# The second-layer coefficients of token blocks 1, 6 and 7 move to a pool of their own, opened after the constants of the attention are closed

## Chip, cores and metric

The kernel runs on one core of one Trainium2 chip. The metric is device microseconds of one execution; the spans and rows below come from one profiled execution. The engines are TensorE (PE: matmuls; PEld: its weight loads), VectorE (DVE), ScalarE (ACT), GpSimd (POOL, which here only issues gathers) and SyncE (SP, which issues the other transfers).

## What is computed

One encoder layer on 1024 tokens of width 1024: two attentions, a gated merge, and a retrieval of single-neuron experts (PEER). The change touches the last part:

```python
def peer(xn, wq, keys, u, v):          # per token: 8 heads x 16 experts = 128 of 16384
    ...                                # top 16 of two key halves, top 16 of their sums -> e, g
    ue = u[e]                          # first layer: 128 rows of 1024 floats per token
    ve = v[e]                          # second layer: 128 rows of 1024 floats per token
    hid = einsum('thkd,td->thk', ue, xb)
    a = gelu(hid) * g
    return einsum('thk,thkd->td', a, ve)
```

## The kernel before

The tokens are eight blocks of 128. For blocks 2 to 5 (`DBLK`) the experts are computed densely: `gates` turns the chosen experts into a matrix of gate values (DVE lines L653 and L663, ACT lines L660, L661 and L671, PE line L669), and `dense_experts` then multiplies by all of `u` and `v` on PE. For blocks 0, 1, 6 and 7 (`SBLK`) `experts(b)` gathers. POOL issues 256 gathers of 128 rows (512 KB each, L803) for a block, in order: 128 from `u`, 128 from `v`. Each `u` gather is reduced on DVE by one instruction (`junk`, L809) to one column of `hid`. When all 128 columns are there, ACT makes `a` = gelu(`hid`) (L811), DVE multiplies it by `g` (L812), and each `v` gather is added by one DVE instruction into `acc` (L815, `acc += a[:,k] * ge`). The gathered tiles `ge` have 5 buffers; a buffer is free again when its DVE instruction is done.

Before the dense stage stand, in this order: the projections with the attention of blocks 0 to 3; the attention of blocks 4 to 7 (`att_rest`: scores L347 on PE, masks and minima L353 on DVE, exponentials L360 on ACT, products L372 on PE); then the merge of blocks 4 and 5 with the gates of blocks 2 and 3 (`mop(2)`); then the choice of experts (`choose`, L559 to L639) of blocks 4 and 5 with the merge of blocks 6 and 7 (`mop(3)`) and the gates of blocks 4 and 5; then the choice for blocks 6 and 7. In a merge, PE (L490) and DVE (L508, L510, L511) take turns, column by column, with two PSUM buffers between them.

`experts` is written last in the program, but nobody queues its instructions by hand: a scheduler lays out every engine's instructions when the program is built, and places the gathers of a block wherever their inputs and buffers are ready. Each engine then runs its own list in order. Memory comes from pools. A pool opened later on the place of a closed one may be written only when the tiles of the closed one have had their last use. `fcon` holds the constants of the attention (`dm`, `nbias`, `far`); it is closed by `fstack.close()` ahead of `dense_experts`, and its last reader is the last L353 of `att_rest`. `gp` is open throughout.

Of the kernel before, what the change touches and what calls it, by code (L numbers as in the profile page):

```python
# [7 lines left out]
F32 = mybir.dt.float32  # L8
# [7 lines left out]
P = 128  # L16
# [17 lines left out]
SBLK = [0, 1, 6, 7]  # L34
# [38 lines left out]
def layer_kernel(ctx, tc, x, w1, w_in, b_gate, lq1, lk1, lq2, lk2, subln, rel,  # L73
# [3 lines left out]
    con = ctx.enter_context(tc.tile_pool(name="con", bufs=1))  # L77
    gp = ctx.enter_context(tc.tile_pool(name="gath", bufs=GBUFS))
    sms = ctx.enter_context(tc.tile_pool(name="sms", bufs=2))
    wp = ctx.enter_context(tc.tile_pool(name="wp", bufs=2))  # L80
    yza = ctx.enter_context(tc.tile_pool(name="yza", bufs=1))
    tkp = ctx.enter_context(tc.tile_pool(name="tkp", bufs=1))
    drp = ctx.enter_context(tc.tile_pool(name="dr", bufs=1, space=bass.MemoryType.DRAM))

    def load(pool, shape, src, name):
# [150 lines left out]
    class Dense:  # L236
# [29 lines left out]
        def run(self):  # L266
            while self.done < len(self.steps):
                self.upto(self.done + 1)
                yield
# [511 lines left out]
    def final(acc, sq, pool, t0, wfb):  # L781
        n = acc.shape[0]
        ss = pool.tile([P, 1], F32, name="ssf", tag="ssf")[:n]
        nc.scalar.activation(sq, acc, AF.Square, accum_out=ss)
        r = rsqrt(pool, ss, 1, 1.0 / D)
        nc.vector.scalar_tensor_tensor(acc, acc, r, wfb[:n], op0=OP.mult, op1=OP.mult)
        nc.sync.dma_start(out[t0:t0 + n, :], acc)

    def experts(b):

        ei, g = idx_of[b]
        K = P
        xs = gp.tile([P, D], F32, name="xs2", tag="xs2", bufs=1)
        nc.sync.dma_start(xs, xn2d[b])
        acc = gp.tile([P, D], F32, name="acc", tag="acc", bufs=1)
        nc.sync.dma_start(acc, hd[b])
        g = g.rearrange("p a b -> p (a b)")
        hid = gp.tile([P, P], F32, name="hid", tag="hid", bufs=1)[:, :K]
        junk = gp.tile([P, D], BF16, name="junk", tag="junk", bufs=1)

        def gather(src, k):
            t = gp.tile([P, D], F32, name="ge", tag="ge")
            nc.gpsimd.indirect_dma_start(out=t, out_offset=None, in_=src,  # L803
                                         in_offset=bass.IndirectOffsetOnAxis(ap=ei[:, k:k + 1], axis=0))
            return t

        for k in range(K):
            t = gather(u, k)
            nc.vector.scalar_tensor_tensor(junk, t, 1.0, xs, op0=OP.mult, op1=OP.mult, accum_out=hid[:, k:k + 1])  # L809
        a = gp.tile([P, P], F32, name="a", tag="a", bufs=1)[:, :K]  # L810
        nc.scalar.activation(a, hid, AF.Gelu)  # L811
        nc.vector.tensor_mul(a, a, g)  # L812
        for k in range(K):
            t = gather(v, k)
            nc.vector.scalar_tensor_tensor(acc, t, a[:, k:k + 1], acc, op0=OP.mult, op1=OP.add)  # L815
        wfb = gp.tile([P, D], F32, name="wfb", tag="ge")
        nc.sync.dma_start(wfb, wf.to_broadcast([P, D]))
        final(acc, junk, sms, b * P, wfb)
# [37 lines left out]
    def sel(blocks, yz):  # L856
        for b in sorted(blocks, key=lambda b: b not in DBLK):
            yield from choose(yz, b)
# [5 lines left out]
    def pool(name):  # L864
        return tc.tile_pool(name=name, bufs=1)
# [29 lines left out]
            weave(mop(3, mp, yza), 26, (chain(sel([4, 5], yzb), gates(gk, d2)), 18 + 32 * len(d2)))  # L895
    fstack.close()
    run(sel([6, 7], yza))
    dense_experts()
    for b in SBLK:
        experts(b)  # L900


# [49 lines left out]
```

## Time and profile before

| | us |
|---|---|
| median of 3 timed runs (lowest, highest) | 3393.28 (3388.62, 3394.96) |
| profiled execution: its time | 3385.27 |
| profiled execution: its span | 3383.5 |
| PE busy (share of the span) | 3101.4 (92%) |
| DVE busy | 2696.5 (80%) |
| ACT busy | 1445.1 (43%) |
| POOL busy | 1249.5 (37%) |

The span is what the records of the profile cover; the execution's own time is 1.8 us longer. Busy shares are means over stages with different limits, so the stages are read one by one.

### The profile page before, as it was taken

Reading aid. Unit: us, or ns where it says so; the run is one execution under the profiler, and the core shown is the slowest. Engines: PE = TensorE matmul, PEld = TensorE weight load, DVE = VectorE, ACT = ScalarE, POOL = GpSimd, SP = SyncE. Lnnn points to the kernel's source line nnn. Section 1 sums busy time; section 2 is a strip of 40 time slices with the busy share of each in tenths; the row PEclk is TensorE's granted clock in tenths of the full one; section 3 lists DMA queues with packets and bytes.
Section 4 is the critical chain, followed back from the end, with each engine's and each line's share of the span. In section 5 each row is a group of like instructions: output and inputs, shape, how many; then the busy total and the mean of one; then the engine's idle time right before and its main releaser. Section 6 shows DMA issues by size and latency. Waiting matters only on the chain.

```text
span 3383.5 us, 48294 instructions
## 1 busy us (share of the span) xinstructions
PE 3101.4 (92%) x16032; PEld 2548.4 (75%) x16032; DVE 2696.5 (80%) x5848; ACT 1445.1 (43%) x3029; POOL 1249.5 (37%) x1028
## 2 busy tenths in 40 slices
PE   7997689999979886987787699999999999999998
PEld 7986578888857664676676578888888888888886
DVE  4436797777769999888885999888888888898843
ACT  5634433434324544567749833333323323322323
POOL 0000455555544532344100035555555555555400
PEclk9998899999989897998898899999999999999999
DMA  7675999999999975898744579999999999999841
GB/s 240 217 243 192 369 323 352 334 355 333 332 340 356 323 269 176 281 325 332 269 152 151 210 265 356 344 336 335 340 335 353 329 335 338 337 343 341 314 128 69
DMA packets 406122, 987.13 MB, mean 292 GB/s; under 512 B 43184, under 2 KB 188400, under 8 KB 403696
## 3 DMA queue, kind: packets, MB, share of 16 engines
q0 software_dynamic: 147456, 536.94, 44.8%
q1 hardware_dynamic: 258416, 447.11, 38.0%
q8 instruction: 126, 2.06, 0.2%
q14 instruction: 124, 1.02, 0.1%
HBM read 905.72 MB, written 78.15 MB: 291 GB/s over the span
## 4 chain that ended last, share of the span: by engine, by line
PE 75%; DVE 12%; DMA 5%; ACT 4%; issue 3%; POOL 1%; SPq 0%; DVEq 0%; POOLq 0%; ACTq 0%
PE ph L136 21%; PE mm L136 17%; PE acc L710 15%; PE mm L490 7%; PE acc L717 5%; PE sc L347 3%; PE pv L372 3%; PE tr L203 2%; DVE junk L809 1%; DMA ge<-in_u_dram,ei 1%; PE gg L669 1%; DVE acc L815 1%; DVE qs L561 1%; DVE iu L563 1%; DVE iu L560 1%
## 5 line engine op out<-in xcount | busy, mean ns | idle before, releaser
L803 POOL DMA_INDIRECT ge<-in_u_dram,ei x512 | 616.7, 1205 | 1258.1 <-DVE junk L809 380.3
L803 POOL DMA_INDIRECT ge<-in_v_dram,ei x512 | 632.6, 1236 | 686.9 <-DVE acc L815 469.3
L815 DVE SCALAR_TENSOR_TENSOR acc<-ge,a,acc 128x1024 f32<-128x1024 f32 x512 | 655.1, 1279 | 21.6 <-DMA ge<-in_v_dram,ei 15.9
L809 DVE SCALAR_TENSOR_TENSOR junk<-ge,xs 128x1024 bf16<-128x1024 f32 x512 | 624.1, 1219 | 50.9 <-DMA ge<-in_u_dram,ei 44.6
L129 DVE TENSOR_TENSOR wl<-wr,wh 128x1024 fp32r<-128x1024 f32 x232 | 283.4, 1222 | 215.8 <-ACT wh L128 110.7
L128 ACT CAST wh<-wr 128x1024 fp32r<-128x1024 f32 x232 | 243.4, 1049 | 404.8 <-PE ph L136 276.5
L136 PE MATMUL ph<-x2h,wh 128*128 128x512 f32 x1024 | 406.2, 397 | 8.8 <-DVE x2l L129 6.6
L136 PE MATMUL ph<-x2l,wh 128*128 128x512 f32 x1024 | 407.7, 398 | 0.0
L136 PE MATMUL mm<-xh,wh 128*128 128x256 f32 (+1 forms) x1248 | 372.1, 325 | 0.7 <-ACT st L286 0.6
L136 PE MATMUL mm<-xl,wh 128*128 128x256 f32 (+1 forms) x1248 | 367.0, 321 | 1.3 <-DVE xl L232 1.2
L136 PE MATMUL ph<-x2h,wl 128*128 128x512 f32 x1024 | 259.4, 395 | 0.0
L136 PEld LDWEIGHTS mm<-xh,wh 128*128 128x128 f32 x1248 | 237.0, 190 | 24.8 <-ACT st L286 3.1
L128 ACT CAST vh<-vr 128x512 fp32r<-128x512 f32 x256 | 140.0, 618 | 269.3 <-PE acc L717 244.5
L136 PEld LDWEIGHTS mm<-xl,wh 128*128 128x128 f32 x1248 | 236.6, 190 | 21.4 <-DVE xl L232 2.0
L136 PEld LDWEIGHTS ph<-x2h,wh 128*128 128x128 f32 x1024 | 193.4, 189 | 55.5 <-DVE x2l L129 7.0
L136 PE MATMUL mm<-xh,wl 128*128 128x256 f32 (+1 forms) x1248 | 234.5, 324 | 0.0
L136 PEld LDWEIGHTS ph<-x2l,wh 128*128 128x128 f32 x1024 | 193.6, 189 | 47.7
L136 PEld LDWEIGHTS ph<-x2h,wl 128*128 128x128 f32 x1024 | 192.0, 188 | 46.9
L347 PE MATMUL sc<-kt,qt 64*128 64x256 f32 (+3 forms) x608 | 200.7, 529 | 14.5 <-DVE mn L353 9.0
L128 ACT CAST ah<-ge 128x512 fp32r<-128x512 f32 x128 | 79.7, 622 | 294.9 <-DVE ge L749 294.9
L710 PE MATMUL acc<-vh,ah 128*128 128x512 f32 x768 | 198.8, 389 | 0.0
L136 PEld LDWEIGHTS mm<-xh,wl 128*128 128x128 f32 x1248 | 184.8, 190 | 16.8
(203 smaller groups left out, 5733.1 us busy)
## 6 DMA issues: line engine op xcount, KB each, us to landing
vr<-in_v_dram SPq DMA_DIRECT2D x128, 512.0 KB, 6.5
wr<-in_ut_dram SPq DMA_DIRECT2D x128, 512.0 KB, 5.8
wr<-in_w_in_dram SPq DMA_DIRECT2D x104, 512.0 KB, 5.3
gdr<-gst SPq DMA_DIRECT2D x16, 2048.0 KB, 8.7
gj<-gdr SPq DMA_DIRECT2D x512, 64.0 KB, 6.0
wr<-in_w_bd_dram SPq DMA_DIRECT2D x40, 512.0 KB, 4.2
wr<-in_w_out_dram SPq DMA_DIRECT2D x40, 512.0 KB, 7.4
wr<-in_wq_dram SPq DMA_DIRECT2D x40, 512.0 KB, 5.1
```

Of the source, the lines that this page charges most:

```text
L128: nc.scalar.copy(hi, raw)
L129: nc.vector.tensor_sub(lo, raw, hi.bitcast(F32))
L136: nc.tensor.matmul(o, w[a][:, k, :], xx[b][:, k, :], start=(i == 0), stop=(i == last))
L203: nc.tensor.transpose(o[:, i * P:(i + 1) * P], s, ident)
L347: nc.tensor.matmul(o[:, :k1 - k0], q, k[:, k0:k1], start=True, stop=True)
L372: nc.tensor.matmul(o[:, :P], aT[:, j - c, :], vt[:, v0 + j, :], start=(j == 0), stop=(j == n - 1))
L490: nc.tensor.matmul(o, w[:, k, :], xx[:, k, :], start=(k == 0), stop=(k == K - 1))
L710: nc.tensor.matmul(acc[i][hf], a[x][:, i * P:(i + 1) * P], b[y][:, hf * 512:hf * 512 + 512], **kw)
L717: nc.tensor.matmul(o, aa[:, 3 * P:4 * P], bb[:, cs], start=(n == 0), stop=(n == len(todo) - 1))
L803: nc.gpsimd.indirect_dma_start(out=t, out_offset=None, in_=src, in_offset=bass.IndirectOffsetOnAxis(ap=ei[:, k:k + 1], axis=0))
L809: nc.vector.scalar_tensor_tensor(junk, t, 1.0, xs, op0=OP.mult, op1=OP.mult, accum_out=hid[:, k:k + 1])
L815: nc.vector.scalar_tensor_tensor(acc, t, a[:, k:k + 1], acc, op0=OP.mult, op1=OP.add)
```

## The change

`a` of block 0 stays in `gp`. `a` of blocks 1, 6 and 7 is taken from a new pool `late`, opened after `fstack.close()`, on the place where `fcon` was. `wp` (the weight buffers) is opened after `yza` and `tkp` instead of ahead of them; all three stay open to the end. No instruction is added or removed apart from one table load on ACT; all else that differs is the order that the scheduler finds.

```diff
@@ layer_kernel
     sms = ctx.enter_context(tc.tile_pool(name="sms", bufs=2))
-    wp = ctx.enter_context(tc.tile_pool(name="wp", bufs=2))
     yza = ctx.enter_context(tc.tile_pool(name="yza", bufs=1))
     tkp = ctx.enter_context(tc.tile_pool(name="tkp", bufs=1))
+    wp = ctx.enter_context(tc.tile_pool(name="wp", bufs=2))
@@ experts
-    def experts(b):
+    def experts(b, late):
...
-        a = gp.tile([P, P], F32, name="a", tag="a", bufs=1)[:, :K]
+        a = late.tile([P, P], F32, name="a", tag="a", bufs=1)[:, :K]
@@ the end of layer_kernel
     fstack.close()
     run(sel([6, 7], yza))
-    dense_experts()
-    for b in SBLK:
-        experts(b)
+    with pool("late") as late:
+        dense_experts()
+        for b in SBLK:
+            experts(b, gp if b == 0 else late)
```

The order of DVE's list shows what that moves. In the end of the attention (`pc` are the score tiles of its last part, `ohib` and `sel` belong to the choice of block 3), DVE's list was, before:

```order
L353 ISA pc_12306,mn<-sc,far 128x384
L353 ISA mn 128x1
L445 RECIPROCAL rz<-z 128x1
L815 SCALAR_TENSOR_TENSOR acc<-ge,a,acc 128x1024
L353 ISA pc_12307,mn<-sc,far 128x384
L353 ISA mn 128x1
L617 TENSOR_TENSOR ohib<-ohib 128x4x128
L353 ISA pc_12306,mn<-sc,nbias,mn 128x256
L353 ISA mn 128x1
L815 SCALAR_TENSOR_TENSOR acc<-ge,a,acc 128x1024
```

and is now:

```order
L353 ISA pc_12306,mn<-sc,far 128x384
L353 ISA mn 128x1
L445 RECIPROCAL rz<-z 128x1
L614 TENSOR_TENSOR ohib<-ohib 128x1024
L617 TENSOR_TENSOR ohib<-ohib 128x4x128
L617 TENSOR_TENSOR ohib<-ohib 128x4x64
L617 TENSOR_TENSOR ohib<-ohib 128x4x32
L619 TENSOR_TENSOR sel<-ohib 128x64
L612 TENSOR_TENSOR ohib<-pos,iotaj 128x1024
L508 SCALAR_TENSOR_TENSOR g_13314<-g_13314,mm 128x256
L614 TENSOR_TENSOR ohib<-ohib 128x1024
L353 ISA pc_12307,mn<-sc,far 128x384
```

The `acc` instructions of block 1 are gone from between the score tiles, and the choice of block 3 has moved up into their places. Where DVE's last L353 of the attention stands (score tile `pc_13185`), the list is now:

```order
L353 ISA pc_13185,mn<-sc,nbias,mn 128x256
L353 ISA mn 128x1
L445 RECIPROCAL rz<-z 128x1 x2
L812 TENSOR_TENSOR a<-a,g 128x128
L815 SCALAR_TENSOR_TENSOR acc<-ge,a,acc 128x1024 x5
L510 SCALAR_TENSOR_TENSOR g_13314<-g_13314,mm 128x256
```

`a` of block 1 is finished right behind the attention's last instruction, and the first `acc` follows it; before, 60 of the block's 128 `acc` stood ahead of this place. On DVE in the choice of block 4 (`sv`, `gs`, `row`), with the merge of blocks 6 and 7 (`mT`, `g_15275`, `g_15346`) beside it, the list was, before:

```order
L625 TENSOR_REDUCE gs<-g 128x8
L599 SCALAR_TENSOR_TENSOR row<-s_15265,s_15264 128x128
L508 SCALAR_TENSOR_TENSOR g_15275<-g_15275,mm 128x256
L559 MAX sv<-cand 128x8 x3
L626 RECIPROCAL gs<-gs 128x8
L559 MAX sv<-cand 128x8 x2
L600 TENSOR_SCALAR s_15265<-row 128x128
```

and is now:

```order
L625 TENSOR_REDUCE gs<-g 128x8
L815 SCALAR_TENSOR_TENSOR acc<-ge,a,acc 128x1024
L511 TENSOR_TENSOR mT<-g_15275 128x256
L599 SCALAR_TENSOR_TENSOR row<-s_15265,s_15264 128x128
L559 MAX sv<-cand 128x8 x3
L626 RECIPROCAL gs<-gs 128x8
L559 MAX sv<-cand 128x8 x5
L508 SCALAR_TENSOR_TENSOR g_15346<-g_15346,mm 128x256
L815 SCALAR_TENSOR_TENSOR acc<-ge,a,acc 128x1024
```

Here `acc` instructions have come in, every eight or so instructions, where before there was none. Counted over DVE's list, the 128 `acc` of block 1 stand so, between the marks named:

| stretch of DVE's list | acc before | acc now |
|---|---|---|
| up to the last L353 of the attention | 60 | 0 |
| P: on to the merge of blocks 6 and 7 (its L496) | 55 | 57 |
| Q: on to the last top-16 (L559) of blocks 4 and 5 | 13 | 16 |
| R: on to the 65th gate (L653), the first of block 4 | 0 | 31 |
| S: on to the 76th gate | 0 | 23 |
| behind it | 0 | 1 |

POOL's list of gathers has the same order as before: blocks 0, 1, 6, 7, each `u` and then `v`.

## Rows read from the trace of the kernel before

**Rows 1.** The page: chain that ended last, and busy tenths in 40 slices

```profile
span 3383.5 us, 48294 instructions
...
DVE  4436797777769999888885999888888888898843
ACT  5634433434324544567749833333323323322323
POOL 0000455555544532344100035555555555555400
...
PE 75%; DVE 12%; DMA 5%; ACT 4%; issue 3%; POOL 1%; SPq 0%; DVEq 0%; POOLq 0%; ACTq 0%
```

**Rows 2.** Windows: stretch, length, busy us (x instructions), granted clock, DMA share, GB/s

```profile
core 0: us, PE busy (x) PEld busy (x) DVE busy (x) ACT busy (x) POOL busy (x), PEclk, DMA share, GB/s
1250.00:1350.00 100.00, 70.72 (x271) 44.13 (x269) 99.52 (x403) 45.32 (x104) 24.17 (x25) 0.74 0.57 169
1350.00:1450.00 100.00, 97.39 (x560) 69.10 (x560) 89.59 (x216) 58.66 (x154) 37.92 (x39) 0.97 0.82 274
1453.50:1600.00 146.50, 114.39 (x678) 101.52 (x679) 122.43 (x213) 107.89 (x254) 62.01 (x51) 0.92 0.91 337
1600.00:1697.00 97.00, 72.98 (x424) 63.62 (x422) 86.75 (x339) 63.21 (x145) 15.91 (x14) 0.85 0.73 265
1697.00:1745.00 48.00, 44.13 (x183) 37.34 (x184) 45.28 (x213) 11.29 (x25) 0.00 (x0) 0.89 0.51 156
1745.00:1772.00 27.00, 23.81 (x140) 20.90 (x139) 17.81 (x51) 22.74 (x53) 0.00 (x0) 1.00 0.33 111
1772.00:1985.00 213.00, 161.85 (x881) 137.33 (x882) 164.64 (x649) 165.12 (x367) 8.41 (x8) 0.85 0.52 188
```

**Rows 3.** Windows of DVE's L815 alone, in the first two stretches

```profile
1250.00:1350.00 100.00, 25.35 (x20) 0.74 0.57 169
1350.00:1450.00 100.00, 49.71 (x39) 0.97 0.82 274
```

**Rows 4.** Waits of PE, 1250 to 1350: total us, times, longest

```profile
PE sc L347 <- DVE mn L353: 8.3, 8, 1.8
PE tr L203 <- DVE p L392: 8.1, 4, 5.7
PE tr L203 <- DVE rz L390: 2.8, 1, 2.8
PE tr L203 <- DVE rz L389: 2.7, 1, 2.7
```

**Rows 5.** Windows: 1000 us of the dense stage

```profile
2100.00:3100.00 1000.00, 1000.00 (x4347) 815.63 (x4346) 886.07 (x1166) 306.56 (x462) 526.06 (x415) 1.00 0.96 339
```

**Rows 6.** Timeline of DVE: start, us, what [idle before]

```profile
1453.09 0.48 DVE L353 CUSTOM_DVE_ANT_0 pc<-sc,nbias,mn 128x256 f32<-128x256 f32 x1
...
1616.21 2.29 DVE L496 TENSOR_TENSOR on<-on,rb 128x2048 f32<-128x2048 f32 x1 [7.75 <-DMA rb<-rst]
...
1691.15 0.85 DVE L559 MAX8 vv<-qs 128x8 f32<-128x128 f32 x4
...
1744.49 1.29 DVE L653 TENSOR_TENSOR o<-iota,it 128x512 f32<-128x512 f32 x2
...
1771.10 0.69 DVE L653 TENSOR_TENSOR o<-iota,it 128x512 f32<-128x512 f32 x1 [2.92 <-PE gg L669]
```

**Rows 7.** Groups of DVE, 1350 to 1450: xcount | busy, mean ns

```profile
L815 DVE SCALAR_TENSOR_TENSOR acc<-ge,a,acc 128x1024 f32<-128x1024 f32 x39 | 49.7, 1275 | 0.0
```

**Rows 8.** Waits of PE, 1600 to 1745; then of DVE, 1745 to 1772

```profile
PE mm L490 <- DVE g L508: 16.6, 2, 14.3
...
DVE o L653 <- PE gg L669: 8.1, 5, 2.9
```

**Rows 9.** Groups of DVE, 1745 to 1772: the gates

```profile
L653 DVE TENSOR_TENSOR o<-iota,it 128x512 f32<-128x512 f32 x10 | 6.8, 689 | 8.1 <-PE gg L669 8.1
L663 DVE TENSOR_SCALAR o<-iota,it 128x128 f32<-128x128 f32 x20 | 6.0, 341 | 0.0
```

**Rows 10.** Timeline of ACT: a table load

```profile
1709.08 1.28 ACT L623 ACT_TABLE_LOAD   x1
```

## Prediction

> **What bounds the kernel now.** I read the page first, for the stages, and then windows of 20 to 200 us between 1200 us and the dense stage, because the order of the lists says that only this part moves. The chain that ended last runs 75% on PE [rows 1], but that is a sum over stages. In the dense stage PE is busy all the time, at full clock, while DVE is busy 886 of 1000 us and the DMA engines 96% [rows 5]; DVE's and POOL's lists there are the same as before, in the main, so I expect this stage only to be shifted. Ahead of it, from 1250 to 1772, DVE is the busiest engine in most stretches. In the diagonal part of the attention's end, 1250 to 1350, it is busy 99.5 of 100 us, while PE is busy 70.7 at a granted clock of 0.74 [rows 2] and waits for DVE in four places, 21.9 us together [rows 4]. From 1350 to 1450 PE is busy 97.4 and DVE 89.6 [rows 2]. Then comes stretch P with 122 of 146.5 us on DVE, Q with 87 of 97, R with 45.3 of 48, and S, where ACT (22.7 of 27) and not DVE (17.8) is the fuller one [rows 2]. DVE is thus near its limit on both sides of the place from which the work is taken, and that decides what moving it is worth.
>
> **What the change moves.** The 60 `acc` ahead of the last L353 leave the attention and stand behind it: 2 more in P, 3 more in Q, 31 more in R, 23 in S, one later (the table above). One takes 1275 ns [rows 7], so 60 x 1.275 = 76.5 us of DVE time leave one stage and enter the next. The sum of DVE's work is unchanged: the kernel wins only if the idle time of DVE shrinks.
>
> **What the attention gains.** In 1250 to 1350 20 `acc` go, 25.3 us [rows 3]. DVE keeps 99.5 - 25.3 = 74.2 us of work, so the stretch can't become shorter than that; PE's waits for DVE were 21.9 us [rows 4], and a chain from scores to minima to exponentials to products remains. I take 19 us (between 10 and 25). In 1350 to 1450 39 go, 49.7 us [rows 3], and DVE keeps only 39.9. But PE was busy 97.4 of 100 [rows 2]; by that the gain is 2.6 us. Busy matmuls overlap, however; PE's weight loads fill 69.1 us here, and 81.6% in the dense stage [rows 5], where PE is never idle. At that density the stretch would take 69.1/0.816 = 84.7 us, a gain of 15.3. I take 8, between the two. The Trainium skill, Perfetto Trace Analysis, section Identifying the Most-Contended Engine, says that matmul busy time does not tell how near TensorE is to its limit and that the share of weight loads does; by that rule alone this term would be 15 and not 8, and by the busy row alone 3. Together the attention's end gains 27 us, with 13 and 40 as its ends. The two ACT table loads at 1.28 us [rows 10] that no longer interrupt the exponentials are hidden, since ACT was busy 104 of 200 us [rows 2].
>
> **What the stages behind it pay.** P, from the last L353 at 1453.1 to the merge's L496 at 1616.2 [rows 6], has 2 more `acc` and one more gate (0.69 + 2 x 0.34 = 1.4 us [rows 9]), 4.0 us in all. DVE was idle 24 of the first 146.5 us [rows 2], so I count 2. Q, to 1691 [rows 6], has 3 more `acc` and one gate fewer: 3.8 - 1.4, so 2.5, since DVE has little idle time there behind the 7.75 us wait at L496 [rows 6]. R, to the 65th gate at 1744.5 [rows 6], is where the price is. The choice of block 4 and the merge of blocks 6 and 7 are both chains through DVE: PE waited there 16.6 us for DVE's L508 [rows 8]. DVE was busy 45.3 of 48 us [rows 2]; with 31 `acc` more it has 45.3 + 39.5 = 84.8, so R grows by at least 36.8. I take 37. What is late next is the first gate of block 4, and with it ACT, which is the fuller engine behind that gate. S, to the 76th gate at 1771.1 [rows 6], has 23 to 24 `acc` more: 17.8 + 24 x 1.275 = 48.4 us of DVE in place of 27, if they fill the 9 us in which DVE was idle (8.1 of them waiting for PE's gates [rows 8]). That is 21. Sum: 2 + 2.5 + 37 + 21 = 62.5. The low end is 48, if P hides its share and the stretch behind S, where DVE is idle 48 of 213 us [rows 2], gives back 10. The high end is 85: 76.5 with no idle time filled, and 8 for gathers that land late.
>
> **The gathers.** R and S together ask for 55 more gathers in 48 + 27 + 58 = 133 us, one in 2.4 us. The dense stage gets one in 1000/415 = 2.41 us, with the DMA engines 96% busy [rows 5]. In R and S the other transfers take 156 and 111 GB/s [rows 2], so the gathers should just keep up. The first 5 lie in their buffers when `a` is finished, as the list shows 5 `acc` in a row there. No other list waits for POOL.
>
> **The rest at nothing.** The new place of `wp` moves addresses of pools that are open to the end either way. `late` adds 512 bytes under the dense stage's pools. Neither adds an instruction to a list. Behind the 76th gate DVE's list is as before, so the dense stage starts later by the sum and ends later by it.
>
> **Sum.** 62.5 - 27 = 35.5, rounded to 35 us. The profiled execution took 3385.3 and spans 3383.5 [rows 1]; it would take 3420. The median of the timed runs is 8 us above that execution, so I put the changed kernel at 3393 + 35 = 3428. The ends of the two terms give 48 - 40 = 8 and 85 - 13 = 72, that is 3401 to 3465: the forecast's own range. A measurement of this kernel can tell about 0.2%, 6.8 us, from no change.
>
> **Rivals.** First, faster: the attention's end was held by DVE alone. Then it loses all 76.5 us and the stages behind pay 62.5, which gives -14: 3379. For it speaks that weight loads fill only 113 of the 200 us (44.1 + 69.1 [rows 2]); against it, that in the second half PE is busy 97.4 and that PE's waits for DVE were all in the first. It decides from a shortening of 69 us on, that is 131 us for what takes 200: chance 0.13.
>
> Second, no change: the stages behind S have 48 us of idle DVE, and if their gates catch up with what S lost, the price falls to 76.5 - 48 = 28.5, which the 27 of the attention pay for: 3395. Against it speaks that the lists behind the 76th gate are the same, and that ACT is busy 165 of 213 there [rows 2]: 0.10. The Trainium skill, Perfetto Trace Analysis, section Optimization Strategy, says that a kernel whose fullest engine changes over time may gain by interleaving its regimes. By that rule the `acc` belong into this stretch, where DVE has room, and not into R, where it has none; the list puts one of them there.
>
> Third, dearer still: the gathers don't keep up. In P, with the DMA engines at 0.91, 51 were issued in 146.5 us, one in 2.87 [rows 2]. At that rate R and S need 158 us and not 133, which adds 25: 3453. In P it was DVE that set the pace, which speaks against it: 0.14.
>
> Fourth, the change does what its name says, and the 128 gathers wait for the dense stage. They would then follow the last one of block 7, at about 3214 (38 of 40 slices [rows 1]), at 2.41 us each: 308 us, past 3520. The list rules that out, since `a` stands right behind the attention: 0.01.
>
> **Chances.** The forecast has 0.62, the others as given. Slower by over 0.2%: 0.62 + 0.14 + 0.01 = 0.77, less 0.01 for the forecast's low end; within 0.2%: 0.10; faster: 0.13 + 0.01. The range runs from 3389 to 3462: it leaves out the faster case and the top of the third.
>
> **What would show it.** After the change, the last L353 of the attention should come at about 1426 (27 earlier), the merge's L496 27 to 25 earlier than 1616.2, the 65th gate about 15 later than 1744.5 and the 76th about 35 later than 1771.1. DVE should be about 70% busy in the attention's end and over 95% between L496 and the 76th gate. The dense stage should be of the same length. If the last L353 comes before 1400, the first rival holds; if L815 waits for its gathers by 10 us or more in R and S, the third. What would make the prediction wrong is PE following DVE in the attention's second half, or R's chain having slack that its 94% busy DVE hides.

## The result, and the profile after

The changed kernel takes 3413.78 us (median of 4 runs, 3412.18 to 3416.25); the kernel before took 3393.58 beside it (4 runs, 3388.62 to 3394.96). The ratio is 1.0063, with a 95% interval of 1.0045 to 1.0080: slower by 20 us. The forecast was 3428, so the sign and the range held, but the size was 14 us too high. The profiled execution took 3414.14 us. Its page answers to [rows 1]:

```profile
span 3412.3 us, 48282 instructions
...
DVE  4436797777769899487996899988998888999843
ACT  5634433334324535567428943333333233333332
POOL 0000455555544530043251015555555555555400
...
PE 73%; DVE 13%; DMA 7%; ACT 4%; issue 3%; POOL 0%; SPq 0%; DVEq 0%; ACTq 0%; POOLq 0%
```

DVE's row has a hole in the 17th slice (4 where it was 8), and 9 in the 20th and 21st, where it was 8. The windows by stretch answer to [rows 2]; here the stretches are cut at the landmarks of this trace (last L353, L496, last L559 of the split keys, first gate of block 4):

```profile
core 0: us, PE busy (x) PEld busy (x) DVE busy (x) ACT busy (x) POOL busy (x), PEclk, DMA share, GB/s
1250.00:1350.00 100.00, 85.10 (x351) 52.98 (x350) 95.54 (x458) 54.14 (x135) 6.61 (x8) 0.74 0.31 96
1350.00:1438.50 88.50, 85.96 (x528) 63.88 (x528) 39.66 (x154) 51.04 (x136) 0.00 (x0) 0.98 0.27 85
1438.50:1600.00 161.50, 129.42 (x745) 114.62 (x745) 134.32 (x226) 116.92 (x273) 70.82 (x57) 0.90 0.88 325
1606.00:1681.00 75.00, 55.96 (x326) 48.52 (x326) 75.00 (x293) 48.08 (x110) 16.34 (x16) 0.88 0.80 290
1681.00:1769.00 88.00, 58.49 (x235) 47.49 (x235) 85.03 (x277) 11.67 (x26) 36.80 (x31) 0.87 0.87 302
1769.00:1819.00 50.00, 23.70 (x107) 20.05 (x108) 46.84 (x81) 26.66 (x59) 25.64 (x20) 0.62 0.77 255
```

In the attention's end DVE is now busy 135.2 of 188.5 us, 72%. Behind L496 it is full: 75.0 of 75, 85.0 of 88, 46.8 of 50, together 97%. The same windows for DVE's L815 alone answer to [rows 3]:

```profile
1250.00:1350.00 100.00, 0.00 (x0) 0.74 0.31 96
1350.00:1439.00 89.00, 0.00 (x0) 0.98 0.27 84
1439.00:1606.00 167.00, 73.08 (x57) 0.91 0.89 329
1606.00:1681.00 75.00, 20.43 (x16) 0.88 0.80 290
1681.00:1769.00 88.00, 39.72 (x31) 0.87 0.87 302
1769.00:1819.00 50.00, 29.51 (x23) 0.62 0.77 255
```

No `acc` is left in the attention's end; R has 31 and S 23. The timeline of DVE at the landmarks answers to [rows 6]:

```profile
1438.29 0.48 DVE L353 CUSTOM_DVE_ANT_0 pc<-sc,nbias,mn 128x256 f32<-128x256 f32 x1
...
1605.85 2.29 DVE L496 TENSOR_TENSOR on<-on,rb 128x2048 f32<-128x2048 f32 x1 [6.63 <-DMA rb<-rst]
...
1768.93 1.29 DVE L653 TENSOR_TENSOR o<-iota,it 128x512 f32<-128x512 f32 x2
```

Then comes what the prediction had not foreseen. Over the instructions of one tile, a row gives the duration (lowest, median, highest) and the first and the last start. For `ph`, the first-layer sums of the dense stage, the kernel before has this row:

```profile
L136 PE MATMUL ph<-x2h,wh x1024: 389/394/796, 1948.1 to 3355.0; 128*128 128x512 f32 x171
```

and the changed kernel this one:

```profile
L136 PE MATMUL ph<-x2h,wh x1024: 387/390/795, 1999.2 to 3383.9; 128*128 128x512 f32 x171
```

The dense stage starts 51.1 us later (about 10 of them lay between these two executions before the first moved instruction, as is shown further down), but from its first to its last such matmul it takes 1384.7 us in place of 1406.9: it gives 22.2 us back. PE is busy all the time in it, in both; what differs is the pace. The timeline of PE, before:

```profile
2301.81 0.39 PE L136 MATMUL ph<-x2h,wh 128*128 128x512 f32 x1
...
2304.85 0.40 PE L136 MATMUL ph<-x2l,wh 128*128 128x512 f32 x1
```

That is 13 steps in 3.04 us, 233.8 ns from one start to the next. After:

```profile
2302.97 0.39 PE L136 MATMUL ph<-x2h,wh 128*128 128x512 f32 x1
...
2304.78 0.39 PE L136 MATMUL ph<-x2h,wh 128*128 128x512 f32 x1
```

Here 8 steps take 1.81 us, 226.3 ns. With 3 x 1024 such matmuls, 7 ns are about 22 us. In the window of [rows 5] the changed kernel accordingly gets through 4414 matmuls, not 4347:

```profile
2100.00:3100.00 1000.00, 1000.00 (x4414) 828.19 (x4413) 898.24 (x1200) 311.50 (x472) 544.68 (x423) 1.00 0.97 345
```

So there are two effects of opposite sign: work moved, and a faster dense stage (about -20 us). The experiments take them apart.

### The profile page after: what moved, and what is told of

Read it like the earlier page. It is cut to its first block, busy times and chain, and to the rows that moved or that the text cites. A ratio compares the mean times of both kernels' runs of the same rounds, so it can differ in the third digit from the quotient of the medians.

```text
span 3412.3 us, 48282 instructions
## 1 busy us (share of the span) xinstructions
PE 3095.4 (91%) x16032; PEld 2559.2 (75%) x16032; DVE 2700.9 (79%) x5848; ACT 1441.8 (42%) x3028; POOL 1273.6 (37%) x1028
## 4 chain that ended last, share of the span: by engine, by line
PE 73%; DVE 13%; DMA 7%; ACT 4%; issue 3%; POOL 0%; SPq 0%; DVEq 0%; ACTq 0%; POOLq 0%
PE ph L136 20%; PE mm L136 16%; PE acc L710 15%; PE mm L490 6%; PE acc L717 5%; PE sc L347 3%; PE pv L372 3%; PE tr L203 2%; DVE junk L809 1%; PE gg L669 1%; DVE acc L815 1%; DMA ge<-in_u_dram,ei 1%; DMA ge<-in_v_dram,ei 1%; ACT gst L671 1%; DVE qs L561 1%
## 5 line engine op out<-in xcount | busy, mean ns | idle before, releaser
L803 POOL DMA_INDIRECT ge<-in_v_dram,ei x512 | 653.9, 1277 | 797.1 <-DVE acc L815 568.3
L815 DVE SCALAR_TENSOR_TENSOR acc<-ge,a,acc 128x1024 f32<-128x1024 f32 x512 | 656.5, 1282 | 34.2 <-DMA ge<-in_v_dram,ei 28.2
L136 PE MATMUL ph<-x2l,wh 128*128 128x512 f32 x1024 | 400.3, 391 | 0.0
L136 PEld LDWEIGHTS ph<-x2h,wh 128*128 128x128 f32 x1024 | 193.2, 189 | 50.5 <-DVE x2l L129 7.8
L347 PE MATMUL sc<-kt,qt 64*128 64x256 f32 (+3 forms) x608 | 193.5, 533 | 12.1 <-DMA qt<-qd 6.3
```

Source lines behind the costliest of these rows:

```text
L136: nc.tensor.matmul(o, w[a][:, k, :], xx[b][:, k, :], start=(i == 0), stop=(i == last))
L347: nc.tensor.matmul(o[:, :k1 - k0], q, k[:, k0:k1], start=True, stop=True)
```

## The experiments

**The two parts, each alone.** `e1_layout_alone` is the kernel before with only the pool moved:

```diff
-    wp = ctx.enter_context(tc.tile_pool(name="wp", bufs=2))
     yza = ctx.enter_context(tc.tile_pool(name="yza", bufs=1))
     tkp = ctx.enter_context(tc.tile_pool(name="tkp", bufs=1))
+    wp = ctx.enter_context(tc.tile_pool(name="wp", bufs=2))
```

> The kernel before with only the pool of the weight buffers laid out behind the pools that stay open; every engine's list of instructions is that of before. The weight buffers of the dense stage (wh, wl) then start at a multiple of 64 bytes of a partition (before: 32 bytes past one); the dense pool keeps its addresses. Theory A (the place of the weights sets the pace of the dense stage's 3072 ph matmuls: in the two traces one starts 233.5 ns after the one ahead of it before, 227 ns after the change): 3072 x 6.6 ns = 20 us less, about 3373 us, ph at 227 ns and the dense stage 20 to 23 us shorter. Rival B (the pace came from the 512 bytes by which the dense pool was shifted by the late buffer): no change, 3389 to 3397 us. Rival C (the order of the gathers, with 60 fewer accumulations left to run beside the dense stage, makes it shorter): no change either.

It took 3379.60 us, against 3396.65 for the kernel before beside it: ratio 0.9951 (0.9937 to 0.9965), 17 us faster. The row of `ph` in its trace:

```profile
L136 PE MATMUL ph<-x2h,wh x1024: 389/389/796, 1961.0 to 3348.7; 128*128 128x512 f32 x171
```

1387.7 us, 19 less than before, with every list as before. Rivals B and C fall. `e2_late_alone` is the reverse, the changed kernel with the pool back in its place:

```diff
+    wp = ctx.enter_context(tc.tile_pool(name="wp", bufs=2))
     yza = ctx.enter_context(tc.tile_pool(name="yza", bufs=1))
     tkp = ctx.enter_context(tc.tile_pool(name="tkp", bufs=1))
-    wp = ctx.enter_context(tc.tile_pool(name="wp", bufs=2))
```

> The changed kernel with the weight buffers' pool back in its old place; the gathers of block 1 still wait for the dense stage's pools, and the dense pool is still shifted by 512 bytes. Theory A (the place of the weights sets the dense stage's pace): the changed kernel's 3414 us plus the 20 us that the dense stage loses again, about 3434 us (3428 to 3442), ph back at 233.5 ns. Rivals B and C (the shift of the dense pool, or the order of the gathers, is what shortened the dense stage): 3412 to 3417 us, ph at 227 ns.

3434.63 us, ratio to before 1.0107 (1.0088 to 1.0126): 38 us slower than before and 21 slower than the whole change. (The `acc` of block 1 do not wait for the dense stage's pools, as the expectation puts it, but for the end of the attention, as the windows of L815 above show.) Its `ph` run from 1999.0 to 3406.0, 1407.0 us, as before. Moving the work alone costs 38 us; moving the pool alone gains 17; the change, 20 us slower, is their sum to within 1 us.

**What about the place counts.** First theory: the start of the weight buffers modulo 64 bytes. `e3_pad_32` adds two unused buffers to the kernel before (the second behind `tkp`):

```diff
+    pad1 = ctx.enter_context(tc.tile_pool(name="pad1", bufs=1))
+    pad1.tile([P, 8], F32, name="pad1t")
     wp = ctx.enter_context(tc.tile_pool(name="wp", bufs=2))
```

> The kernel before, the pools in their old order, with an unused buffer of 32 bytes in a partition ahead of the weight buffers' pool and one behind the last open pool. The weight buffers start at a multiple of 64 bytes, only 32 bytes from where they were; so do the buffers behind them; the dense pool is shifted by 64 bytes and stays at a multiple of 64. Theory A1 (what counts is the start of the weights modulo 64): about 3373 us, ph at 227 ns, as in the kernel with the pool moved. Rival A2 (what counts is the region of the memory in which they lie): no change, 3389 to 3397 us, ph at 233.5 ns.

3383.58 us, ratio 0.9959 (0.9945 to 0.9973), between the kernel before (3396.65) and `e1_layout_alone` (3379.60). The row of `ph` (here at L140) gives 1393.5 us, 13 of the 22 us:

```profile
L140 PE MATMUL ph<-x2h,wh x1024: 388/392/792, 1959.8 to 3353.3; 128*128 128x512 f32 x171
```

The region of the memory (A2) is thus not what counts, but modulo 64 is not the whole of it either. `e4_moved_and_pad` adds the same two lines ahead of `wp` in the changed kernel, and the second buffer behind it:

> The changed kernel, whole, with an unused buffer of 32 bytes ahead of the weight buffers' pool and one behind it: the weights lie in their new place but 32 bytes past a multiple of 64, the dense pool at a multiple of 64. Theory A1 (the start of the weights modulo 64 sets the pace): about 3434 us (3428 to 3442), ph back at 233.5 ns. Rival A2 (their region of the memory): 3412 to 3417 us, ph at 227 ns.

3433.29 us, ratio to before 1.0106 (1.0090 to 1.0123), `ph` from 1996.2 to 3403.2, 1407.0 us. The gain is gone, in the new place. `f1_dense_32` then asked which operand it is, with one line in the kernel of `e1_layout_alone`:

```diff
     dk = st.enter_context(tc.tile_pool(name="dk", bufs=2))
+    dk.tile([P, 8], F32, name="dkpad", bufs=1)
```

> The kernel with only the weight buffers' pool moved (3380 us), with an unused buffer of 32 bytes at the head of the dense pool: x2h, x2l, vh, vl, ah and al all start 32 bytes past a multiple of 64, the weights wl and wh stay at a multiple. It asks which operand's start sets the pace of a dense matmul of 512 columns (227 or 233.5 ns from one start to the next). Theory S (the stationary operand's: wl and wh for ph, ah and al for acc): ph stays at 227, the 3072 acc matmuls go to 233.5, 20 us more, about 3400 us. Theory M (the moving operand's: x2h and x2l for ph, vh and vl for acc; what helped before would then be something else): both at 233.5, 40 us more, about 3420. Theory D (that the two operands start differently modulo 64): ph at 233.5, acc at 227, about 3400. Theory N (no start matters, the region does): 3380.

3396.65 us, ratio 1.0008 (0.9999 to 1.0018): the gain of the moved pool is gone, though the weights stay where they are. `ph` is slow,

```profile
L136 PE MATMUL ph<-x2h,wh x1024: 392/394/794, 1959.1 to 3366.1; 128*128 128x512 f32 x171
```

while `acc`, both of whose operands start 32 bytes past a multiple of 64 in this kernel, shows a median of 389 ns, that of `ph` at the fast pace:

```profile
L711 PE MATMUL acc<-vl,ah x768: 389/389/393, 1978.0 to 3376.3; 128*128 128x512 f32 x192
```

That is theory D: the distance of the two operands counts. The first theory fell. What its period is took four more kernels, each with one unused buffer at the same line. `g1_dense_96` puts 96 bytes into the kernel before (`[P, 24]` in that line), `g2_dense_128` 128 bytes into that of `e1_layout_alone` (`[P, 32]`):

> The kernel before, the weight buffers in their old place, with an unused buffer of 96 bytes at the head of the dense pool. x2h, x2l, wl and wh then all start 96 bytes past a multiple of 128 (before: x2h and x2l at a multiple, wl and wh 96 past one). Theory D (what counts is whether the two operands of a matmul start alike modulo 128): ph at 227 ns in place of 233.5, about 20 us less than before, 3373 us (3370 to 3380), and the dense stage as short as in the kernel with the pool moved. Rival A1 (an operand that starts off a multiple of 64 is read more slowly): ph at 233.5 ns or more, 3389 us or more.

> The kernel with only the weight buffers' pool moved, with an unused buffer of 128 bytes at the head of the dense pool: all operands at a multiple of 64, the weights and x2h alike modulo 128 but 128 apart modulo 256. Theory D with 128 bytes as the period: nothing changes, ph at 227 ns, about 3380 us. Theory D with a period of 256 or 512: ph above 228 ns, and 5 to 20 us more, 3385 to 3400 us.

`g1_dense_96` took 3397.26 us (ratio 1.0009, 0.9998 to 1.0020), `g2_dense_128` 3400.13 (1.0021, 1.0011 to 1.0031). In both the dense stage is slow, 1407.9 and 1408.6 us; the row of `g2_dense_128`:

```profile
L136 PE MATMUL ph<-x2h,wh x1024: 389/395/792, 1960.2 to 3368.8; 128*128 128x512 f32 x171
```

With 128 as the period theory D fell as well, and the forecast of 3373 with it. `g3_dense_480` puts 480 bytes into the kernel before (`[P, 120]`), `g4_dense_256` 256 bytes into that of `e1_layout_alone` (`[P, 64]`):

> The kernel before, the weight buffers in their old place, with an unused buffer of 480 bytes at the head of the dense pool, so that x2h starts a multiple of 512 bytes behind wl (before: 32 bytes more than a multiple), while every operand still starts off a multiple of 64. Theory D512 (the pace of ph follows the distance of the two operands modulo 512: 0 gives 227 ns, 64 gives 229, 128 and 32 give 233): ph at 227 ns, the dense stage at 1398 to 1401 us in place of 1420, about 3375 us (3370 to 3382). Rival A (both operands have to start at a multiple of 64, and at the same one modulo 256): ph at 232 ns or more, the dense stage at 1420 us, 3389 us or more.

> The kernel with only the weight buffers' pool moved, with an unused buffer of 256 bytes at the head of the dense pool: x2h starts 256 bytes more than a multiple of 512 behind wl. Theory D512 (period 512): ph above 228 ns and the dense stage between 1405 and 1422 us, 3385 to 3400 us. Theory D256 (period 256): ph at 227 ns, the dense stage at 1398 to 1401 us, about 3380 us.

These two expectations count the dense stage to its last `acc` (1420 us in the kernel before), the text to the last `ph` of the rows (1406.9). `g3_dense_480` took 3375.63 us, ratio 0.9944 (0.9931 to 0.9958):

```profile
L136 PE MATMUL ph<-x2h,wh x1024: 389/389/796, 1961.2 to 3348.8; 128*128 128x512 f32 x171
```

`g4_dense_256` took 3379.07, ratio 0.9956 (0.9942 to 0.9971), and is as fast in the dense stage:

```profile
L136 PE MATMUL ph<-x2h,wh x1024: 387/389/796, 1962.5 to 3349.4; 128*128 128x512 f32 x171
```

So no operand has to start at a multiple of 64 (in `g3_dense_480` none does), no buffer has to be moved, and all distances tried fit a period of 256 bytes: 256 more changes nothing, 128 more does. All kernels in one table; the starts are bytes of a partition as the programs lay their buffers out, the last column is worked out from the rows of `ph`. The buffers of `wh`, `wl`, `x2h` and `x2l` lie multiples of 256 bytes from one another within their pools, so one distance holds for all three kinds of `ph`.

| kernel | `wl` | `x2h` | distance modulo 256 | first to last `ph`, us |
|---|---|---|---|---|
| before | 73312 | 110720 | 32 | 1406.9 |
| `e2_late_alone` | 73312 | 111232 | 32 | 1407.0 |
| `e4_moved_and_pad` | 94368 | 111296 | 32 | 1407.0 |
| `f1_dense_32` | 94336 | 110752 | 32 | 1407.0 |
| `e3_pad_32` | 73344 | 110784 | 64 | 1393.5 |
| `g1_dense_96` | 73312 | 110816 | 128 | 1407.9 |
| `g2_dense_128` | 94336 | 110848 | 128 | 1408.6 |
| after | 94336 | 111232 | 0 | 1384.7 |
| `f4_moved_left_out` | 94336 | 111232 | 0 | 1386.0 |
| `e1_layout_alone` | 94336 | 110720 | 0 | 1387.7 |
| `g3_dense_480` | 73312 | 111200 | 0 | 1387.6 |
| `g4_dense_256` | 94336 | 110976 | 0 | 1386.9 |
| `f3_all_aligned` | 94400 | 110784 | 0 | 1386.6 |

The traces give the steps themselves too. Between 2050 and 3300 us the mean step from the start of one `ph` to that of the next is 226.7 ns in all six kernels at distance 0, 229.0 at 64, 233.3 in all four at 32 and 232.8 in both at 128; from one `acc` to the next it is 226.7 to 227.6 in all thirteen. At 32, nine in ten steps of `ph` take 231 ns or more, so the time does not come from a few long delays. Each run moves a whole pool, the raw weights with the split ones; that nearly every step of `ph` is longer, and hardly any of `acc`, is what points to the operands of `ph` itself.

**The rest of the matmuls.** `f3_all_aligned` is `e1_layout_alone` with an unused `[P, 8]` buffer in `con`, one ahead of `wp` and one at the head of `fcon`:

```diff
+    con.tile([P, 8], F32, name="conpad")
     iota = con.tile([P, P], F32, name="iota")
...
+    fc.tile([P, 8], F32, name="fcpad")
     dm = fc.tile([P, S], F32, name="dm")
```

> The kernel with only the weight buffers' pool moved, with three unused buffers of 32 bytes (among the constants, ahead of the weight buffers' pool, and at the head of the attention's constants), so that the operands of the attention, the merge and the choice start at a multiple of 64 bytes as well; gather buffers too. If the same rule holds for the matmuls ahead of the dense stage: some 7000 of them with 128 to 512 columns, most of them in stretches that another engine holds; 3365 to 3378 us, with the dense stage as long as in the kernel it is made from. If the start matters only for wh and wl: 3377 to 3384 us. A time above 3390 would say that a multiple of 64 costs something elsewhere.

3371.91 us, ratio 0.9940 (0.9926 to 0.9953). That is the lowest time here, but its interval overlaps those of `e1_layout_alone` and `g3_dense_480`; whether the stages ahead gain anything is not settled. All three beat both kernels.

**The price of the moved work.** `f4_moved_left_out` is the changed kernel without the last 60 accumulations of block 1 and their gathers:

```diff
-        for k in range(K):
+        for k in range(K - 60 if b == 1 else K):
             t = gather(v, k)
```

> The changed kernel without the last 60 of the 128 accumulations of block 1's second layer (and their gathers); that part of the sum is left out, so the output lacks it. In the changed kernel these are the ones that run from about 1650 us on, in stretches R and S. The forecast's price for R and S (37 and 21 us): 3414 - 58 = 3356 us (3350 to 3362), the dense stage starting 58 us earlier. Rival (R and S are held by the chain of choices and merges over PE and ACT, and DVE's added work only fills gaps; the shift came from elsewhere): less than 30 us, 3385 us or more. Rival (they cost their whole DVE time and push the stage behind S too): 76 us, 3338 us.

3356.96 us, 57 less than the changed kernel (ratio to before 0.9887, 0.9872 to 0.9903). Its landmarks on DVE:

```profile
1610.11 2.29 DVE L496 TENSOR_TENSOR on<-on,rb 128x2048 f32<-128x2048 f32 x1 [6.85 <-DMA rb<-rst]
...
1731.78 1.28 DVE L653 TENSOR_TENSOR o<-iota,it 128x512 f32<-128x512 f32 x2
```

Its row of `ph`:

```profile
L136 PE MATMUL ph<-x2h,wh x1024: 389/389/795, 1942.9 to 3328.9; 128*128 128x512 f32 x171
```

From L496 to the first gate it needs 121.7 us, where the changed kernel needs 163.1: 41.4 for Q and R (forecast 2.5 + 37). From there to the first `ph` 211.1 against 230.3: 19.2 for S and what follows (forecast 21). Of the 60, 36 had stood in Q and R (the forecast counts 34 there) and 24 behind them. Both rivals fall: the 60 cost far more than 30 us, and less than their 76.5 us of DVE. With them gone the scheduler also orders some of the rest differently (the last steps of block 1 on ACT come earlier, for one), so the 57 us are the price of the 60, their gathers and that order together.

## Why the prediction was right and wrong

For the terms the right partner is `e1_layout_alone`, which has the lists of before and the layout of after. The profiled execution of before ran ahead of its own median by 8 us: in the attention of blocks 4 to 7, with no instruction moved so far, one pair of L353 starts at 1227.25 in before (1237.14 and 1236.90 in the two others):

```profile
1227.25 0.75 DVE L353 CUSTOM_DVE_ANT_0 p<-sc,dm,mn 128x512 f32<-128x512 f32 x1
1231.38 0.73 DVE L353 CUSTOM_DVE_ANT_0 p<-sc,dm,mn 128x512 f32<-128x512 f32 x1
```

The timeline of DVE in `e1_layout_alone`, with the first of that pair ahead:

```profile
1237.14 0.75 DVE L353 CUSTOM_DVE_ANT_0 p<-sc,dm,mn 128x512 f32<-128x512 f32 x1
...
1464.66 0.48 DVE L353 CUSTOM_DVE_ANT_0 pc<-sc,nbias,mn 128x256 f32<-128x256 f32 x1
...
1628.66 2.29 DVE L496 TENSOR_TENSOR on<-on,rb 128x2048 f32<-128x2048 f32 x1 [7.66 <-DMA rb<-rst]
...
1756.53 1.28 DVE L653 TENSOR_TENSOR o<-iota,it 128x512 f32<-128x512 f32 x2
```

And the pair's first in the changed kernel:

```profile
1236.90 0.75 DVE L353 CUSTOM_DVE_ANT_0 p<-sc,dm,mn 128x512 f32<-128x512 f32 x1
```

**The attention's end**: from that pair to the last L353 227.5 us become 201.4, a gain of 26.1; the forecast was 27. Its two halves held as well. DVE runs the L353 in the same order in all three kernels, so one of them can serve as the boundary that the prediction drew at 1350. In the kernel before it is this one:

```profile
1352.32 0.56 DVE L353 CUSTOM_DVE_ANT_0 pc<-sc,far 128x384 f32<-128x384 f32 x1 [0.31 <-PE tr L203]
```

The same instruction in `e1_layout_alone`

```profile
1362.22 0.56 DVE L353 CUSTOM_DVE_ANT_0 pc<-sc,far 128x384 f32<-128x384 f32 x1 [0.31 <-PE tr L203]
```

and in the changed kernel

```profile
1343.34 0.56 DVE L353 CUSTOM_DVE_ANT_0 pc<-sc,far 128x384 f32<-128x384 f32 x1
```

Up to it 18.6 us are gained (forecast 19) and behind it 7.5 (forecast 8); by the eight L353 around it the first figure lies between 16 and 20, so the split is good to about 2 us. For the second part the rule of the Trainium skill that the prediction weighed (Perfetto Trace Analysis, section Identifying the Most-Contended Engine: judge TensorE by its weight loads, not by its matmul busy time) gave 15 and the busy row 3; the measured 7.5 lies between them. The trace agrees with the rule in part: PE's busy share stayed at 97% (97.39 of 100 us, then 85.96 of 88.5) though the stretch became shorter, but the weight loads fill 72% of it now (63.88 of 88.5), not the 82% of the dense stage. DVE now waits for PE there (before, 1.9 us at this place from 1350 to 1450), as the waits of DVE from 1250 to 1440 show (line, what it waited for, total us, times, longest):

```profile
DVE pc L353 <- PE tr L203: 28.3, 17, 3.3
```

**P, Q, R and S**: P grew from 164.0 us to 167.6 (3.6, forecast 2), Q and R from 127.9 to 163.1 (35.2, forecast 39.5), and the way from the first gate to the first `ph` from 204.5 to 230.3 (25.8, forecast 21). In sum 64.6, where 62.5 was forecast; R's price goes with the moved `acc`, as `f4_moved_left_out` showed. The single terms were off by 4 to 5 us in opposite directions, and part of that is order: without the 60, Q and R are 6.2 us shorter than in `e1_layout_alone` (121.7 against 127.9, with 2 `acc` fewer) and the way to the first `ph` is 6.6 longer (211.1 against 204.5). In S the granted clock is 0.62 where it was 1.00 [rows 2], after PE had been busy 58.5 of 88 us; in `f4_moved_left_out` it is 1.00 there (1731.8 to 1770). How much of the 25.8 that makes no run separates. Against `e1_layout_alone` L496 comes 22.8 us earlier (forecast 27 to 25), the first gate 12.4 later (forecast 15), and the first `ph`, which stands in for the 76th gate here because some records of gates are missing, 38.2 later (forecast 35). The two medians lie 34.2 us apart, but they come from different sets of runs; each against the kernel before in its own set, the moved work costs 20.2 + 17.1 = 37.3, and 38.0 by `e2_late_alone`. The forecast's sum was 35.5. Two slips in the prediction changed nothing: the low end of the price, with the shares that it names, is 62.5 - 2 - 10 = 50.5 and not 48, and the range's top of 3462 lies under the 3465 that the forecast's own sum gives.

**The gathers** kept up, as forecast. The waits of DVE from L496 to 1820:

```profile
DVE acc L815 <- DMA ge<-in_v_dram,ei: 4.6, 6, 1.0
```

4.6 us, under the 10 from which the third rival would have held. The first rival falls with an attention shortened by 26 us and not 69; the second with the stretch behind the first gate, which gave nothing back; the fourth with the list.

**The step that failed** is "The rest at nothing": that the new place of `wp` moves addresses only. It moves the weights against the operands they are multiplied with. `yza` and `tkp` together fill 21024 bytes, 32 more than a multiple of 256. Ahead of the change they lay between the weights and the dense pool and put the distance off by 32; behind it the weights lie next to the dense pool, and the 512 bytes of `late` change nothing modulo 256. "The dense stage should be of the same length" was wrong by 22 us of 1407, which the prediction had no term for. 3393 + 35 - 20 would have been 3408, against 3413.78 measured: the moved work cost 2 us more than forecast, and the pool's new place is worth 17 us in the medians. The time came out within the range because the price of the moved work was sized well; the 20 us that were missed lay inside the range's width.

## What to carry to other kernels

When a change moves a pool, work out the distance between the stationary and the moving operand of the matmuls that fill the longest stage; here an unused buffer of 480 bytes gained 18 us where the change of order cost 38. When work of the engine that is fullest on both sides is moved from one stage to the next, price it in each by that engine's idle time: here the sum came out within 3 us and each term within 5. Compare traces against a kernel that has one part of the change alone, and count from an instruction ahead of the first moved one, since executions of one and the same kernel lay up to 14 us apart (the kernel before in the set of `g1_dense_96`, 3388.81 to 3403.21).

## What the runs showed of the hardware

The pace of a matmul of 512 columns (4 bytes each) against a stationary operand of 128 columns, back to back at full clock, depended on the distance of the two operands' starts modulo 256 bytes: at 0 a new one started every 227 ns, at 64 every 229, at 32 and at 128 every 233; the dense stage of 3072 such matmuls, beside as many `acc` at a distance that never changed, took 1385 to 1388 us at 0, 1393.5 at 64, 1407 at 32 and 1408 to 1409 at 128. Their absolute starts, tried at five places of the weights and nine of `x2h`, made no difference that shows. The Trainium skill, SBUF — State Buffer, section Operand start alignment, asks only that an operand start at a multiple of its element size, and says that this is about legality and not speed; its section Who interferes with whom gives TensorE two independent read ports, one for the moving operand and one for weight loads. No run here speaks against the first; the speed differed all the same. As to the second, a pace that hangs on the distance of the two operands does not look like two independent reads. Whether it is these two reads that disturb each other, or what else in the memory does, no run here shows; other distances and the matmuls of 128 and 256 columns were not measured.
